# One packed stream for the input and the first weights, and eight warm-up products, at the start of a decoder-trunk kernel

## The chip, the cores and the metric

The kernel runs on one core of a Trainium2 chip, in one launch. The metric is the device time of that launch in microseconds (us). A core has a matrix engine (TensorE, PE in the rows), whose loading of stationary operands is listed apart (PEld), a vector engine (VectorE, DVE), a scalar engine (ScalarE, ACT), a general engine (GpSimd, POOL) and an engine that here only issues transfers (SyncE, SP). Sixteen DMA engines carry the transfers of all queues.

## The reference

The reference is a decoder trunk of two layers over 256 tokens of width 1024, in float32. Layer 0 has full causal attention with 16 heads of 64 (at this length its block-sparse form has one block); layer 1 has sliding-window attention with learned sinks over 4 shared key/value heads. Each is followed by a gated feed-forward part with a causal convolution of width 3.

```
for l in range(2):
    h = rmsnorm(x, attn_norm[l])
    q, k, v = ...                       # layer 0: h @ w_qkv_a; layer 1: own q, shared k and v
    q, k = partial_rope(q), partial_rope(k)
    x = x + attention(q, k, v) @ w_o
    x = x + conv_ffn(rmsnorm(x, ffn_norm[l]), w_up[l], conv_w[l], conv_b[l], w_down[l])
return rmsnorm(x, final_norm)
```

What matters here is the first 40 us: the first normalization, the value half `v` of the first eight heads, and the query and key group of the first four heads.

## The kernel before

**Products.** Each float32 product is made of three products of rounded parts: every operand is split into a high part (rounded, made by ScalarE or VectorE) and a low part (the operand less its high part, made by VectorE). One step of 128 inputs thus takes three products for each of the two token blocks of 128. Tokens are the stationary side, 512 weight columns the moving side.

**Weights.** All weights lie in DRAM as 1 MB units of 128 x 2048 values, in the order of use. A unit is fetched by SP into one of three raw buffers (`fetch`, L151), then split in two or four pieces: `hi_part` (L156) on ScalarE, `lo_part` (L159) on VectorE. The last low piece frees the raw buffer, and the fetch of the unit after next-but-one follows. Units 0 and 1 are the first value half, units 2 and 3 the first query/key group, 4 and 5 the second, 6 and 7 the third.

**Start.** The input lies in DRAM twice: by token (`x`), and transposed, as eight chunks of 128 features x 256 tokens, behind a column of gains (`xg`). `get_x` (L201) and `get_w` (L208) fetch chunks and quarter units: the first two chunks of x on ScalarE's queue, the rest on SP's, x and weights in turn. `warm_up` (L244) multiplies a tile of ones by itself, with no use of the result, six times. `first_parts(c)` (L764) scales and splits chunk c of x and splits its quarter unit; `v_first(c)` (L725) then issues the six products of chunk c. The first parts of x are not yet normalized: the scale of each token is applied when results are copied out, so it has to be known only there.

**What follows the start on the in-order engines.** ScalarE: the high parts of units 2 and 3, then a sine (L801) for the rotary tables, four squares of the input rows (L292, for the normalization), two copies of the value accumulators (`v_out`, L735), then the high parts of units 4 and 5 and the copies of the first query/key group (`qk_out`, L854). GpSimd makes the angles: positions are fetched to `pos_i` (L710), converted (L747), and some twenty small operations on 16 columns end with L763; VectorE takes an absolute value (L798), GpSimd adds a constant (L799), and the sine follows. VectorE: the low parts of units 2 and 3, that absolute value, then the low parts of units 4 and 5 and the rotation of the first group (`rope`, L339: L343, twice L348, L349). Only then can TensorE transpose the rotated group (`to_feature`, L355), four transposes for each token block.

**Who sets the order.** Up to the first attention the order on TensorE, ScalarE and VectorE is that of the code (`manual_schedule`, L703); the steps of splitting, copying and rotating are put into that order by a simple clock that counts the products' nominal time (`tick`, `chain`). From the first attention on a scheduler orders all engines by its own estimates.

```
def part(i, c):
    hi_part(i, c)
    lo_part(i, c)
...
warm_up(6)
for c in range(4):
    first_parts(c)
    v_first(c)
fetch(3)
```

Of the kernel before, what the change touches and what calls it, by code (L numbers as in the profile page):

```python
# [7 lines left out]
F32 = mybir.dt.float32  # L8
F32R = mybir.dt.float32r
I32 = mybir.dt.int32  # L10
AF = mybir.ActivationFunctionType
ALU = mybir.AluOpType
AX = mybir.AxisListType

P = 128
D = 1024
S = 256
NB = S // P
KC = D // P
# [10 lines left out]
UNIT = 2048  # L30
# [27 lines left out]


@with_exitstack  # L60
def trunk(ctx: ExitStack, tc, x, xg, pos, cpk, fin, sinks, w, out):
    nc = tc.nc
    one = ctx.enter_context(tc.tile_pool(name="one", bufs=1))
    qd = ctx.enter_context(tc.tile_pool(name="qd", bufs=15))
    wk = ctx.enter_context(tc.tile_pool(name="wk", bufs=2))
    wp = ctx.enter_context(tc.tile_pool(name="wp", bufs=4))
# [4 lines left out]
    def nm(s):  # L71
        uid[0] += 1
        return f"{s}_{uid[0]}"
# [3 lines left out]
    SKIP, ROUND = 4, 64  # L77

    def spaced(pool, n, dt, tag, name, bufs):
        return pool.tile([P, n + ROUND], dt, tag=tag, name=name, bufs=bufs)[:, SKIP:SKIP + n]  # L80

    def quad(dt=F32R, name="q"):
        return spaced(qd, 4 * S, dt, "q", nm(name), 15).rearrange("p (c t) -> p c t", c=4)
# [7 lines left out]
    def bank(tag):  # L91
        return ps.tile([P, 512], F32, tag=tag, name=nm(tag), bufs=4 if tag == "acc" else 2)

    def f(ap):
        return ap.bitcast(F32)

    def blk(b):
        return slice(b * P, (b + 1) * P)
# [46 lines left out]
    wq = {}  # L145
    done = [0]

    raws = {}
    w_time = [0.0]

    def fetch(i):  # L151
        if i < N_UNITS:
            raws[i] = wp.tile([P, UNIT], F32, tag="raw", name=f"wr{i}", bufs=3)
            nc.sync.dma_start(raws[i], w[i])

    def hi_part(i, c):  # L156
        nc.scalar.activation(wq[i][0][:, c], raws[i][:, c], AF.Copy)  # L157

    def lo_part(i, c):  # L159
        nc.vector.tensor_tensor(out=wq[i][1][:, c], in0=raws[i][:, c], in1=f(wq[i][0][:, c]), op=ALU.subtract)  # L160

    def weights(i):
        wq[i] = (spaced(wp, UNIT, F32R, "hi", f"wh{i}", 4),
                 spaced(wp, UNIT, F32R, "lo", f"wl{i}", 4))
# [29 lines left out]

    x0t = qd.tile([P, 4 * S + ROUND], F32, tag="q", name="x0a", bufs=15)
    x0 = [x0t[:, KC:KC + 4 * S].rearrange("p (c t) -> p c t", c=4), quad(F32, "x0b")]
    g0 = x0t[:, :KC]

    def get_x(q, c, n):  # L201
        if c == 0:
            q.dma_start(x0t[:, :KC + n * S], xg[:, :KC + n * S])
        else:
            q.dma_start(x0[c // 4][:, c % 4:c % 4 + n],
                        xg[:, KC + c * S:KC + (c + n) * S].rearrange("p (c t) -> p c t", c=n))

    def get_w(i, j, n=1):  # L208
        if j == 0:
            raws[i] = wp.tile([P, UNIT], F32, tag="raw", name=f"wr{i}", bufs=3)  # L210
        c = slice(j * 512, (j + n) * 512)
        nc.sync.dma_start(raws[i][:, c], w[i][:, c])

    get_x(nc.scalar, 0, 1)
    get_x(nc.scalar, 1, 1)
    get_w(0, 0)
    get_w(0, 1)

    cp = one.tile([P, NCOL], F32, name="cp")
    pos_i = one.tile([P, NB], I32, name="pos_i")  # L220
# [6 lines left out]
    xr = [one.tile([P, D], F32, name=f"xr{b}") for b in range(NB)]  # L227

    rb = one.tile([P, S], F32, name="rb")
    one.tile([P, 56], F32, name="pad")  # L230


    ident = one.tile([P, P], F32, name="ident")
# [6 lines left out]
    for b in range(NB):  # L240
        t = one.tile([P, NH, HD], F32, name=f"v{b}")
        v_sb.append(t)

    def warm_up(n):  # L244

        if n:
            t = bank("u")
            for _ in range(int(n)):
                nc.tensor.matmul(t[:, :P], ones, ones, start=True, stop=True)
# [4 lines left out]
    def new_hT():  # L254

        return [(quad(), quad()) for _ in range(2)]
# [47 lines left out]
    def hx(hT, c):  # L304
        hi, lo = hT[c // 4]
        return hi[:, c % 4], lo[:, c % 4]
# [382 lines left out]
    def row_bcast(rb, b):  # L689
# [4 lines left out]
        def spread():  # L694
# [7 lines left out]

    manual = ExitStack()  # L703
    manual.enter_context(tc.manual_schedule(engines={mybir.EngineType.PE, mybir.EngineType.Activation,
                                                     mybir.EngineType.DVE}))


    hT = new_hT()
    get_x(nc.sync, 2, 2)
    nc.sync.dma_start(pos_i, pos)  # L710
    get_w(0, 2)
    get_w(0, 3)
    get_x(nc.sync, 4, 2)
    get_w(1, 0)
    get_w(1, 1)
    get_x(nc.sync, 6, 2)
    get_w(1, 2)
    get_w(1, 3)
    get_w(2, 0, 4)
    weights(0)  # L720
    weights(1)
    rs = []
# [2 lines left out]
    def v_first(c):  # L725
        xh, xl = hx(hT, c)
        s_ = slice((c % 4) * 512, (c % 4 + 1) * 512)
        wh, wl = (t[:, s_] for t in wq[c // 4])
        for k, (a, m) in enumerate(((xh, wh), (xl, wh), (xh, wl))):
            for b in range(NB):  # L730
                nc.tensor.matmul(v_acc[b], a[:, blk(b)], m, start=(c == 0 and k == 0), stop=(c == KC - 1 and k == 2))  # L731
        tick(1280)
# [23 lines left out]
    src = ang  # L756
    for c in (TWO_PI_1, TWO_PI_2, TWO_PI_3):
        for k in (kh, kl):
            nc.gpsimd.tensor_scalar(out=kk, in0=k, scalar1=-c, scalar2=None, op0=ALU.mult)
            nc.gpsimd.tensor_tensor(out=rr, in0=kk, in1=src, op=ALU.add)  # L760
            src = rr
    arg = rb[:, 80:112].rearrange("p (k b d) -> p k b d", k=2, b=NB)
    nc.gpsimd.tensor_scalar(out=arg[:, 0], in0=rr, scalar1=PI_IN, scalar2=-PI_IN, op0=ALU.min, op1=ALU.max)  # L763
    def first_parts(c):  # L764
        hi, lo = hx(hT, c)
        src, g = x0[c // 4][:, c % 4], g0[:, c:c + 1]
        s_ = slice((c % 4) * 512, (c % 4 + 1) * 512)
        if c == 0:
            nc.vector.tensor_copy(wq[0][0][:, s_], raws[0][:, s_])
        nc.scalar.activation(hi, src, AF.Copy, scale=g)  # L770
        if c > 0:
            hi_part(c // 4, s_)
        nc.vector.scalar_tensor_tensor(out=lo, in0=src, scalar=g, in1=f(hi), op0=ALU.mult, op1=ALU.subtract)
        lo_part(c // 4, s_)

    warm_up(6)
    for c in range(4):
        first_parts(c)
        v_first(c)
    fetch(3)  # L780
    nc.sync.dma_start(xr[0], x[blk(0)])
    for c in range(4, KC):
        first_parts(c)
        if c < KC - 1:
            v_first(c)
# [18 lines left out]
    for h in range(2):  # L804
        c = slice(h * HALF, (h + 1) * HALF)
# [216 lines left out]
def pack(inp):  # L1022

    import numpy as np

    def k_major(m):
        return m.reshape(m.shape[0] // P, P, m.shape[1])

    units = []
    m = k_major(inp["w_qkv_a"][0])  # L1030
    q, k, v = (m[:, :, i * D:(i + 1) * D] for i in range(3))
    qk = [np.concatenate([q[:, :, g * 256:(g + 1) * 256], k[:, :, g * 256:(g + 1) * 256]], axis=2) for g in range(4)]
    blocks = [v[:, :, :512], qk[0], qk[1], qk[2], v[:, :, 512:], qk[3]]

    def halves(blk):
        for a in range(2):
            units.append(blk[4 * a:4 * a + 4].transpose(1, 0, 2).reshape(P, UNIT))

    def rows2(mat):
        mm = k_major(mat)  # L1040
        for i in range(mm.shape[0] // 2):
            units.append(mm[2 * i:2 * i + 2].transpose(1, 0, 2).reshape(P, UNIT))

    def up(mat):
        mm = k_major(mat).reshape(KC, P, 2, NF, P)
        for i in range(NF):
            units.append(mm[:, :, :, i].transpose(1, 0, 2, 3).reshape(P, UNIT))

    for blk in blocks:
        halves(blk)  # L1050
    rows2(inp["w_o_a"][0])
    up(inp["w_up"][0])
    rows2(inp["w_down"][0])
    halves(k_major(inp["w_kv_b"]))

    order = [(2 * (j // 4) + e) * 4 + j % 4 for j in range(NH // 2) for e in range(2)]
    m = k_major(inp["w_q_b"][0].reshape(D, NH, HD)[:, order].reshape(D, D))
    for g in range(4):
        units.append(m[:, :, g * 256:(g + 1) * 256].transpose(1, 0, 2).reshape(P, UNIT))
    rows2(inp["w_o_b"][0].reshape(NH, HD, D)[order].reshape(D, D))  # L1060
    up(inp["w_up"][1])
    rows2(inp["w_down"][1])
    assert len(units) == N_UNITS
    wpk = np.stack(units)

    def feat(v_):
        return v_.reshape(-1, P).T

    cols = [feat(v_) for v_ in (inp["kv_norm"], inp["attn_norm"][1],
                                inp["ffn_norm"][0], inp["ffn_norm"][1])]  # L1070
    for l in range(2):
        four = np.concatenate([inp["conv_w"][l], inp["conv_b"][l][None]], axis=0)
        cols.append(four.reshape(4, 2 * NF, P).transpose(2, 1, 0).reshape(P, 2 * NF * 4))
    cpk = np.concatenate(cols, axis=1)
    return {
        "x": inp["x"].reshape(S, D),
        "xg": np.concatenate([feat(inp["attn_norm"][0]), inp["x"].reshape(S, KC, P).transpose(2, 1, 0).reshape(P, D * S // P)],
                             axis=1),
        "pos": inp["positions"].reshape(NB, P).T,
        "cpk": cpk,  # L1080
        "fin": inp["final_norm"],
        "sinks": inp["sinks_b"].reshape(NH)[order],
        "w": wpk,
    }
# [19 lines left out]
```

## Time and profile before

| | before |
|---|---|
| median of 3 runs | 586.36 us (586.33 to 586.93) |
| profiled execution | 587.05 us, of it a span of 585.1 us from first to last instruction |
| TensorE busy | 575.0 us, 98% |
| VectorE, ScalarE, GpSimd busy | 430.1, 381.9, 106.3 us |
| moved by DMA | 101.00 MB, mean 173 GB/s |
| TensorE clock granted, mean of the span | 0.998 |

The span is one execution as the hardware profiler saw it. "Busy" of TensorE includes products whose ends are modelled, so that a row of back-to-back products counts as fully busy; how fast they run is read from the distance of their starts.

### The profile page before, as it was taken

What the parts mean: (1) busy time and instruction counts of PE and PEld (TensorE: products, weight loads), DVE (VectorE), ACT (ScalarE), POOL (GpSimd) and SP (SyncE); (2) the same over time, 40 slices, a digit from 0 to 9 for tenths busy, and PEclk for the clock granted to TensorE, in tenths of its full rate; (3) what the DMA queues carried; (4) which work ended last, traced back from release to release, by engine and by line L of the source; (5) the groups of instructions that cost most, each with busy time, mean ns of one, the idle gap of its engine ahead of it and who ended that gap; (6) DMA issues with size and microseconds to landing.
All of it is one profiled execution on the core that took longest, in us unless ns stands there. A gap on an engine that the chain in (4) does not pass through costs nothing.

```text
span 585.1 us, 10179 instructions
## 1 busy us (share of the span) xinstructions
PE 575.0 (98%) x3854; PEld 508.0 (87%) x3854; DVE 430.1 (74%) x928; ACT 381.9 (65%) x768; POOL 106.3 (18%) x124
## 2 busy tenths in 40 slices
PE   8999999999999999999999999999999999999995
PEld 7887777789999999988888977679999999988884
DVE  5598668589977767677669778669987676777714
ACT  5798767578566566565459588758765665656513
POOL 5430001012222222321003000000222223232003
PEclk9999999999999999999999999999999999999999
DMA  8964543314555454548744522243364545446701
GB/s 282 371 225 149 212 144 144 144 38 180 216 171 190 150 211 145 190 171 286 289 143 143 218 73 72 73 145 145 117 244 151 204 150 188 174 160 235 288 0 72
DMA packets 16320, 101.00 MB, mean 173 GB/s; under 512 B 2064, under 2 KB 2448, under 8 KB 4752
## 3 DMA queue, kind: packets, MB, share of 16 engines
q1 hardware_dynamic: 15840, 99.83, 47.6%
q8 instruction: 30, 0.49, 0.3%
q10 hardware_dynamic: 432, 0.53, 0.3%
q14 instruction: 18, 0.15, 0.1%
HBM read 99.30 MB, written 1.05 MB: 172 GB/s over the span
## 4 chain that ended last, share of the span: by engine, by line
PE 65%; DVE 13%; ACT 9%; POOL 7%; issue 5%; DMA 1%; POOLq 0%; DVEq 0%; ACTq 0%
PE acc L520 9%; PE acc L525 9%; PE acc L521 9%; POOL m L652 7%; PE acc L315 5%; PE acc L316 4%; PE acc L317 4%; DVE m L647 4%; DVE m L645 4%; ACT m L641 4%; DVE wl L160 3%; PE t L474 3%; PE acc L731 2%; PE t L453 2%; PE u L404 2%
## 5 line engine op out<-in xcount | busy, mean ns | idle before, releaser
L160 DVE TENSOR_TENSOR wl<-wr,wh 128x1024 fp32r<-128x1024 f32 (+1 forms) x208 | 224.6, 1098 | 33.8 <-ACT wh L157 33.5
L157 ACT ACTIVATE wh<-wr 128x1024 fp32r<-128x1024 f32 (+1 forms) x207 | 192.2, 960 | 32.8 <-PE acc L525 17.1
L652 POOL TENSOR_TENSOR m<-m,m 128x256 f32<-128x256 f32 x44 | 67.6, 1538 | 205.6 <-DVE m L647 177.5
L520 PE MATMUL acc<-wh,q 128*128 128x512 f32 x238 | 94.4, 397 | 0.0
L521 PE MATMUL acc<-wl,q 128*128 128x512 f32 x238 | 92.9, 390 | 0.0
L608 PE MATMUL u<-q,wh 128*128 128x256 f32 x320 | 88.5, 278 | 0.0
L609 PE MATMUL u<-q,wh 128*128 128x256 f32 x320 | 88.0, 275 | 0.0
L610 PE MATMUL u<-q,wl 128*128 128x256 f32 x320 | 88.0, 275 | 0.0
L608 PE MATMUL t<-q,wh 128*128 128x256 f32 x288 | 79.4, 276 | 0.6 <-DVE m L647 0.6
L609 PE MATMUL t<-q,wh 128*128 128x256 f32 x288 | 79.2, 275 | 0.0
L610 PE MATMUL t<-q,wl 128*128 128x256 f32 x288 | 79.2, 275 | 0.0
L525 PE MATMUL acc<-wh,q 128*128 128x512 f32 x238 | 78.9, 392 | 0.0
L656 ACT ACTIVATE q<-m 128x256 fp32r<-128x256 f32 x44 | 18.4, 418 | 82.4 <-POOL m L652 82.4
L608 PEld LDWEIGHTS u<-q,wh 128*128 128x128 f32 x320 | 59.9, 188 | 0.3 <-issue 0.2
L609 PEld LDWEIGHTS u<-q,wh 128*128 128x128 f32 x320 | 60.1, 188 | 0.0
L610 PEld LDWEIGHTS u<-q,wl 128*128 128x128 f32 x320 | 60.1, 188 | 0.0
L315 PE MATMUL acc<-wh,q 128*128 128x512 f32 (+1 forms) x160 | 57.1, 358 | 0.0
L316 PE MATMUL acc<-wl,q 128*128 128x512 f32 (+1 forms) x160 | 56.2, 351 | 0.0
L317 PE MATMUL acc<-wh,q 128*128 128x512 f32 (+1 forms) x160 | 55.9, 349 | 0.0
L608 PEld LDWEIGHTS t<-q,wh 128*128 128x128 f32 x288 | 54.1, 188 | 1.0 <-issue 1.0
L610 PEld LDWEIGHTS t<-q,wl 128*128 128x128 f32 x288 | 54.1, 188 | 0.0
L609 PEld LDWEIGHTS t<-q,wh 128*128 128x128 f32 x288 | 54.1, 188 | 0.0
(153 smaller groups left out, 1028.5 us busy)
## 6 DMA issues: line engine op xcount, KB each, us to landing
wr<-in_w SPq DMA_DIRECT2D x90, 1024.0 KB, 4.8
wr<-in_w SPq DMA_DIRECT2D x8, 256.0 KB, 5.1
xr<-in_x SPq DMA_DIRECT2D x2, 512.0 KB, 9.1
out<-m SPq DMA_DIRECT2D x3, 256.0 KB, 2.1
x0b<-in_xg SPq DMA_DIRECT2D x2, 256.0 KB, 5.2
fin_t<-in_fin SPq DMA_DIRECT2D x1, 512.0 KB, 5.6
x0a<-in_xg SPq DMA_DIRECT2D x1, 256.0 KB, 5.4
out<-m ACTq DMA_DIRECT2D x1, 256.0 KB, 2.1
```

The lines of the kernel that those rows point to most:

```text
L157: nc.scalar.activation(wq[i][0][:, c], raws[i][:, c], AF.Copy)
L160: nc.vector.tensor_tensor(out=wq[i][1][:, c], in0=raws[i][:, c], in1=f(wq[i][0][:, c]), op=ALU.subtract)
L315: nc.tensor.matmul(o, xh[:, blk(b)], wh, start=(c == 0), stop=False)
L316: nc.tensor.matmul(o, xh[:, blk(b)], wl, start=False, stop=False)
L317: nc.tensor.matmul(o, xl[:, blk(b)], wh, start=False, stop=(c == KC - 1))
L520: nc.tensor.matmul(o, ph[:, blk(b)], hi[:, s_], start=first, stop=False)
L521: nc.tensor.matmul(o, ph[:, blk(b)], lo[:, s_], start=False, stop=False)
L525: nc.tensor.matmul(o, pl[:, blk(b)], hi[:, s_], start=False, stop=end)
L608: nc.tensor.matmul(o, hi[:, s_], xh, start=(c == 0), stop=False)
L609: nc.tensor.matmul(o, hi[:, s_], xl, start=False, stop=False)
L610: nc.tensor.matmul(o, lo[:, s_], xh, start=False, stop=(c == KC - 1))
L652: nc.gpsimd.tensor_tensor(out=h, in0=gs, in1=t[1], op=ALU.mult)
```

## The change

The transposed input and units 0 and 1 lie side by side in one array `xw`: the column of gains, then for each chunk its 256 tokens and its 512 weight columns, 768 values a row. Eight chunks come in seven transfers on SP's queue (chunks 4 and 5 together), into the three raw buffers and two other tiles, issued one behind the other ahead of everything else. Nothing is fetched on ScalarE's queue at the start any more. Unit 2 has no raw buffer of its own now and is fetched once chunks 0 and 1 are split, unit 3 once chunks 2 and 3 are. The gains are copied to a tile of their own (`g1`), because the buffer they come in is used again. SP joins the engines whose order is that of the code, and the warm-up has eight products.

```diff
-    get_x(nc.scalar, 0, 1)
-    get_x(nc.scalar, 1, 1)
-    get_w(0, 0)
-    get_w(0, 1)
+    CH = S + 512
+    first = [wp.tile([P, UNIT], F32, tag="raw", name=f"first{i}", bufs=3) for i in range(3)]
+    first += [qd.tile([P, 4 * S + ROUND], F32, tag="q", name=nm("first"), bufs=15) for _ in range(2)]
...
+    def get_chunks(c, n=1):
+        t, at = (first[c // 2], KC * (c == 1) + c % 2 * CH) if c < 6 else (first[c - 3], 0)
+        lo, hi = c * CH + KC * (c > 0), (c + n) * CH + KC
+        nc.sync.dma_start(t[:, at:at + hi - lo], xw[:, lo:hi])
+
+    for c in range(4):
+        get_chunks(c)
+    get_chunks(4, 2)
+    get_chunks(6)
+    get_chunks(7)
+    g0 = first[0][:, :KC]
+    g1 = one.tile([P, KC], F32, name="g1")
...
-    manual.enter_context(tc.manual_schedule(engines={mybir.EngineType.PE, mybir.EngineType.Activation,
-                                                     mybir.EngineType.DVE}))
+    manual.enter_context(tc.manual_schedule(engines={mybir.EngineType.PE, mybir.EngineType.Activation,
+                                                     mybir.EngineType.DVE, mybir.EngineType.SP}))
...
-    get_x(nc.sync, 2, 2)
     nc.sync.dma_start(pos_i, pos)
-    get_w(0, 2)
-    get_w(0, 3)
-    get_x(nc.sync, 4, 2)
...
-    get_w(2, 0, 4)
...
+            nc.vector.tensor_copy(g1, g0)
...
-    warm_up(6)
+    warm_up(8)
     for c in range(4):
         first_parts(c)
         v_first(c)
-    fetch(3)
+        if c % 2:
+            fetch(2 + c // 2)
```

The order of instructions moves at three places that matter below. In the names, `wr5` is the raw buffer of unit 5, `wh5` and `wl5` its high and low parts, `m2` the two tiles of the first query/key group (token blocks 0 and 1), `t` a bank that takes transposes, `acc` an accumulator.

The first is the head of SP's queue. Before:

```order
L212 DMA wr0_74<-in_w 128x512 x2
L205 DMA x0a_70<-in_xg 128x512
L710 DMA pos_i_78<-in_pos 128x2
L212 DMA wr0_74<-in_w 128x512 x2
L205 DMA x0b_1_71<-in_xg 128x512
L212 DMA wr1_107<-in_w 128x512 x2
```

and now:

```order
L210 DMA first0_70<-in_xw 128x776
L210 DMA first0_70<-in_xw 128x768
L210 DMA first1_71<-in_xw 128x768 x2
L210 DMA first2_72<-in_xw 128x1536
L210 DMA first_1_73<-in_xw 128x768
L210 DMA first_2_74<-in_xw 128x768
L710 DMA pos_i_84<-in_pos 128x2
```

The positions were the fourth transfer of this queue and are now the eighth, behind all chunks.

The second is VectorE where it reaches the first rotation (lines move by one: L343 is now L344, and so on). Before:

```order
L160 TENSOR_TENSOR wl5_373<-wr5_247,wh5_372 128x512
L343 TENSOR_TENSOR rb_87<-m2_21_375,cs_265 128x128
L348 TENSOR_TENSOR rb_87<-m2_21_375,sn_266 128x8x8 x2
L349 TENSOR_TENSOR m2_21_375<-rb_87 128x8x16
L160 TENSOR_TENSOR wl5_373<-wr5_247,wh5_372 128x512
L343 TENSOR_TENSOR rb_87<-m2_22_376,cs_265 128x128
L348 TENSOR_TENSOR rb_87<-m2_22_376,sn_266 128x8x8 x2
L160 TENSOR_TENSOR wl5_373<-wr5_247,wh5_372 128x512
L349 TENSOR_TENSOR m2_22_376<-rb_87 128x8x16
```

and now:

```order
L160 TENSOR_TENSOR wl5_372<-wr5_246,wh5_371 128x512 x4
L344 TENSOR_TENSOR rb_93<-m2_22_374,cs_264 128x128
L349 TENSOR_TENSOR rb_93<-m2_22_374,sn_265 128x8x8 x2
L160 TENSOR_TENSOR wl6_431<-wr6_258,wh6_430 128x1024
L350 TENSOR_TENSOR m2_22_374<-rb_93 128x8x16
L344 TENSOR_TENSOR rb_93<-m2_23_375,cs_264 128x128
L349 TENSOR_TENSOR rb_93<-m2_23_375,sn_265 128x8x8 x2
L160 TENSOR_TENSOR wl6_431<-wr6_258,wh6_430 128x1024
L350 TENSOR_TENSOR m2_23_375<-rb_93 128x8x16
```

The first rotation stood behind one quarter of unit 5 and now stands behind all four; half of unit 6 has moved in ahead of the last step of each rotation.

The third is TensorE, where it transposes what was rotated. Before (16 products of units 4 and 5 stand ahead of the first transposes):

```order
L355 MATMUL t_27_416<-ident_89,m2_21_375 128x128 x4
L315 MATMUL acc_25_380<-wh5_372,q_4_100 128x512
L316 MATMUL acc_25_380<-wl5_373,q_4_100 128x512
L317 MATMUL acc_25_380<-wh5_372,q_5_101 128x512
L315 MATMUL acc_25_380<-wh5_372,q_4_100 128x512
L316 MATMUL acc_26_381<-wl4_340,q_2_98 128x512
L317 MATMUL acc_26_381<-wh4_339,q_3_99 128x512
L316 MATMUL acc_25_380<-wl5_373,q_4_100 128x512
L355 MATMUL t_28_421<-ident_89,m2_22_376 128x128 x4
```

and now (15 products ahead):

```order
L356 MATMUL t_28_415<-ident_95,m2_22_374 128x128 x4
L316 MATMUL acc_26_379<-wh5_371,q_5_106 128x512
L317 MATMUL acc_26_379<-wl5_372,q_5_106 128x512
L318 MATMUL acc_26_379<-wh5_371,q_6_107 128x512
L356 MATMUL t_29_420<-ident_95,m2_23_375 128x128 x4
```

The second transposes stood seven products behind the first and now stand three behind them. Later differences of order end some 290 instructions into TensorE's 3,660; from there the two programs are alike.

## Rows read from the trace of the kernel before

**Rows 1.** Waits of TensorE, whole span: us in total, times, longest.
```profile
PE t L355 <- DVE m L349: 0.6, 1, 0.6
```

**Rows 2.** Timeline of TensorE, the start: start us, us, engine, line, instruction.
```profile
1.11 2.93 PE L249 MATMUL u<-ones 128*128 128x128 f32 x12 [1.11 <-DVE warm L225]
5.00 2.07 PE L731 MATMUL acc<-wh,q 128*128 128x512 f32 x4 [0.96 <-ACT q L770]
...
9.44 0.68 PE L731 MATMUL acc<-wl,q 128*128 128x512 f32 x2
...
17.66 0.61 PE L731 MATMUL acc<-wl,q 128*128 128x512 f32 x2
```

**Rows 3.** Timeline of TensorE, at the first transposes of the rotated group.
```profile
29.14 0.61 PE L315 MATMUL acc<-wh,q 128*128 128x512 f32 x2
...
32.77 0.60 PE L355 MATMUL t<-ident,m 128*128 128x128 f32 x4
...
34.81 0.60 PE L355 MATMUL t<-ident,m 128*128 128x128 f32 x4
```

**Rows 4.** Stretches: length, each engine's busy time, clock, DMA share, GB/s.
```profile
0.00:6.00 6.00, 3.93 (x14) 3.46 (x15) 1.62 (x5) 1.99 (x3) 1.88 (x16) 1.00 0.60 168
6.00:14.85 8.85, 8.85 (x33) 7.15 (x32) 6.25 (x13) 6.66 (x14) 6.69 (x15) 1.00 0.99 360
2.50:12.00 9.50, 8.54 (x30) 6.83 (x29) 6.49 (x13) 6.35 (x13) 4.45 (x9) 1.00 0.95 303
12.00:22.00 10.00, 10.00 (x45) 8.09 (x44) 6.96 (x13) 6.46 (x12) 5.73 (x16) 1.00 1.02 420
30.00:570.00 540.00, 538.66 (x3701) 478.01 (x3701) 407.13 (x876) 357.46 (x716) 86.22 (x71) 1.00 0.47 167
```

**Rows 5.** Timeline of GpSimd, from the positions' landing to the angles.
```profile
7.32 0.48 POOL L747 CAST rb<-pos_i 128x2 f32<-128x2 int32 x1 [4.80 <-DMA pos_i<-in_pos]
7.74 0.95 POOL L826 MEMSET kd<- 128x1024 f32 x1
...
10.22 0.31 POOL L838 MEMSET mask<- 128x256 f32 x1
...
11.31 0.42 POOL L839 TENSOR_SCALAR_AFFINE_SELECT mask<-mask 128x128 f32<-128x128 f32 x1
...
18.49 0.52 POOL L763 TENSOR_SCALAR rb<-rb 128x16 f32<-128x16 f32 x1
```

**Rows 6.** Timeline of ScalarE, from unit 2 to units 4 and 5.
```profile
16.97 2.20 ACT L157 ACTIVATE wh<-wr 128x512 fp32r<-128x512 f32 x4 [1.55 <-DMA wr<-in_w]
19.45 2.20 ACT L157 ACTIVATE wh<-wr 128x512 fp32r<-128x512 f32 x4 [0.29 <-DMA wr<-in_w]
23.02 0.23 ACT L801 ACTIVATE rb<-rb 128x32 f32<-128x32 f32 x1 [1.37 <-POOL rb L799]
...
24.84 0.63 ACT L292 ACTIVATE m<-xr 128x512 f32<-128x512 f32 x1 [0.36 <-DMA xr<-in_x]
...
27.81 2.71 ACT L157 ACTIVATE wh<-wr 128x512 fp32r<-128x512 f32 x5
```

**Rows 7.** Timeline of VectorE, around the absolute value and the first rotation.
```profile
22.54 0.17 DVE L798 SCALAR_TENSOR_TENSOR rb<-rb 128x16 f32<-128x16 f32 x1
...
28.47 3.10 DVE L160 TENSOR_TENSOR wl<-wr,wh 128x512 fp32r<-128x512 f32 x5 [1.92 <-ACT wh L157]
31.49 0.29 DVE L343 TENSOR_TENSOR rb<-m,cs 128x128 f32<-128x128 f32 x1
...
32.08 0.29 DVE L349 TENSOR_TENSOR m<-rb 128x128 f32<-128x128 f32 x1
...
37.69 1.22 DVE L160 TENSOR_TENSOR wl<-wr,wh 128x1024 fp32r<-128x1024 f32 x1
```

**Rows 8.** Stretches at the end of the span, columns as in rows 4.
```profile
578.50:582.50 4.00, 0.00 (x0) 0.00 (x0) 2.24 (x8) 1.31 (x4) 1.27 (x2) 1.00 0.27 100
583.00:583.50 0.50, 0.00 (x0) 0.00 (x0) 0.00 (x0) 0.00 (x0) 0.00 (x0) 0.50 0.65 242
```

More of the change, by code (lines that the diff above doesn't have):

```diff
@@ L60, in trunk @@
 @with_exitstack
-def trunk(ctx: ExitStack, tc, x, xg, pos, cpk, fin, sinks, w, out):
+def trunk(ctx: ExitStack, tc, x, xw, pos, cpk, fin, sinks, w, out):
     nc = tc.nc
@@ L193, in need, with chunk @@
         require("w", i)
[L197 to L212, printed above, removed]
-    get_x(nc.scalar, 0, 1)
-    get_x(nc.scalar, 1, 1)
-    get_w(0, 0)
-    get_w(0, 1)
+    CH = S + 512
+    first = [wp.tile([P, UNIT], F32, tag="raw", name=f"first{i}", bufs=3) for i in range(3)]
+    first += [qd.tile([P, 4 * S + ROUND], F32, tag="q", name=nm("first"), bufs=15) for _ in range(2)]
+    def chunk(c):
+        t, at = (first[c // 2], KC * (c < 2) + c % 2 * CH) if c < 6 else (first[c - 3], 0)
+        return t[:, at:at + S], t[:, at + S:at + CH]
+    def get_chunks(c, n=1):
[9 more added lines that the diff above has]
+    g1 = one.tile([P, KC], F32, name="g1")
     cp = one.tile([P, NCOL], F32, name="cp")
@@ L229, in trunk @@
     rb = one.tile([P, S], F32, name="rb")
-    one.tile([P, 56], F32, name="pad")
+    one.tile([P, 48], F32, name="pad")
     ident = one.tile([P, P], F32, name="ident")
@@ L704, in trunk @@
     manual.enter_context(tc.manual_schedule(engines={mybir.EngineType.PE, mybir.EngineType.Activation,
-                                                     mybir.EngineType.DVE}))
+                                                     mybir.EngineType.DVE, mybir.EngineType.SP}))
     hT = new_hT()
-    get_x(nc.sync, 2, 2)
     nc.sync.dma_start(pos_i, pos)
-    get_w(0, 2)
-    get_w(0, 3)
-    get_x(nc.sync, 4, 2)
[L714 to L718, printed above, removed]
-    get_w(2, 0, 4)
     weights(0)
@@ L765, in first_parts @@
         hi, lo = hx(hT, c)
-        src, g = x0[c // 4][:, c % 4], g0[:, c:c + 1]
-        s_ = slice((c % 4) * 512, (c % 4 + 1) * 512)
+        (src, raw), g = chunk(c), (g1 if c > 1 else g0)[:, c:c + 1]
+        wh, wl = (t[:, (c % 4) * 512:(c % 4 + 1) * 512] for t in wq[c // 4])
         if c == 0:
-            nc.vector.tensor_copy(wq[0][0][:, s_], raws[0][:, s_])
+            nc.vector.tensor_copy(wh, raw)
+            nc.vector.tensor_copy(g1, g0)
         nc.scalar.activation(hi, src, AF.Copy, scale=g)
         if c > 0:
-            hi_part(c // 4, s_)
+            nc.scalar.activation(wh, raw, AF.Copy)
         nc.vector.scalar_tensor_tensor(out=lo, in0=src, scalar=g, in1=f(hi), op0=ALU.mult, op1=ALU.subtract)
-        lo_part(c // 4, s_)
-    warm_up(6)
+        nc.vector.tensor_tensor(out=wl, in0=raw, in1=f(wh), op=ALU.subtract)
+    warm_up(8)
     for c in range(4):
@@ L1076, in pack @@
         "x": inp["x"].reshape(S, D),
-        "xg": np.concatenate([feat(inp["attn_norm"][0]), inp["x"].reshape(S, KC, P).transpose(2, 1, 0).reshape(P, D * S // P)],
-                             axis=1),
+        "xw": np.concatenate([feat(inp["attn_norm"][0])] + [
+            t for c in range(KC) for t in (inp["x"].reshape(S, KC, P)[:, c].T, blocks[0][c])], axis=1),
         "pos": inp["positions"].reshape(NB, P).T,
```

## The prediction

> **What bounds the kernel now.** I read the stretches first. From 30 to 570 us TensorE is busy 538.7 of 540 us [rows 4]: the kernel is one stream of products, and what delays the stream early is not made up later. The list of TensorE's waits then tells where the stream ever stops: besides the first microseconds it holds little, but one of its rows is a transpose (L355) that waits 0.6 us for the last step of a rotation on VectorE [rows 1]. So a late rotation does stop TensorE, since it works strictly in order there.
>
> The timeline of the start shows the second thing. The six warm-up products (twelve rows) take 2.93 us and end at 4.04; TensorE idles 0.96 us; from 5.00 to 9.44 it does ten products, 0.444 us each; the 36 from 9.44 to 17.66 take 0.228 us each [rows 2]. 512 columns in 0.43 to 0.44 us are the 1.2 GHz level, half of the later pace, although the clock column shows 1.00 in these stretches [rows 4]. Had the higher level been there from 5.00, ten products would cost 2.2 us less. That is the most that the start can give.
>
> Third, the stretch of the first transposes. From 29.14, 16 products and then four transposes: 32.77 less 29.14, over 16, is 0.227 us a product, so nothing waits; the second transposes at 34.81 come seven products later, which leaves 0.45 us for the four transposes between [rows 3]. On VectorE the last step of the first rotation runs at 32.08 to 32.37 [rows 7]: 0.4 us before it is needed. This is a small margin, and behind it stands a long chain: positions landed at 7.32, angles done at 18.49 + 0.52 = 19.01 [rows 5], absolute value 22.54 [rows 7], sine 23.02, squares, first high part of unit 4 at 27.81 [rows 6], first low part 28.47, rotation 31.49 [rows 7].
>
> **The change, part by part.**
>
> *Warm-up.* Eight products take 8/6 of 2.93, 3.9 us, and end at 5.0, about where the first real product starts now [rows 2]. No time is added; the idle 0.96 us is filled, and the higher clock may come up to 4.4 us earlier. Worth between 0 and 2.2 us at the start; I take 1.5. It is spent before 33 us, as follows.
>
> *Chunks in one queue.* The bytes are the same: 3.15 MB of x and units 0 and 1. Now 168 GB/s for 6.0 us and 360 for the next 8.85 us move 1.01 and 3.19 MB; the mean from 2.5 to 12 is 303, from 12 to 22 it is 420 [rows 4]. With longer rows and no second queue I expect the later pace once the first 1.01 MB are in: 2.14 MB at 420 GB/s take 5.1 us, the last chunk has moved at 11.1. TensorE needs 8 x 6 x 0.228 = 10.9 us from 5.0 at the high clock, so it is just kept fed. The copy of the gains is 128 x 8 values, and lies where VectorE waits for ScalarE: nothing.
>
> *Positions behind the chunks.* In bytes the positions stood behind 1.05 MB (four chunks of x, two quarter units), which had moved at 6.1; they landed at 7.32 [rows 5], 1.2 us after. Unit 2 ends at 4.20 MB, moved at 14.85 [rows 4], and was taken at 16.97 [rows 6], 2.1 us after. The positions now stand behind 3.15 MB: they land at 11.1 + 1.2 = 12.3. The fast bound is 420 GB/s from 2.5, 11.2; the slow one 303 GB/s from 2.5 and 2.1 us, 15.0.
>
> *GpSimd's angles.* From landing to end 11.7 us now, of which the fills L826, L838 and L839 take 0.95 + 0.31 + 0.42 = 1.7 [rows 5]; they now come before the landing. That leaves 10.0, so the angles end at 22.3, not 19.0. Absolute value to sine is 23.02 - 22.54 = 0.5: the sine runs at 22.8 (21.7 to 25.5). Its other releaser is VectorE's work on unit 3: the sine follows that unit's first high part by 23.02 - 19.45 = 3.6 [rows 6]. Unit 3 lies 2.1 MB behind the chunks: 11.1 + 5.0 + 2.1 = 18.2, sine 21.8. So the positions decide, by 1 us, and the faster transfers bring the sine hardly forward (23.0 to 22.8).
>
> *Rotation later in the order.* Here the new order costs. From sine to the first high part of unit 4 now 4.79, of it 0.36 a wait for the input rows [rows 6]; without that 4.4. First low part 0.66 later, and five take 31.49 - 28.47 = 3.02, so 0.60 each [rows 7]. Eight of them, not five, stand ahead of the rotation: 4.83. First two steps of the rotation 0.59, half of unit 6 1.22, last step 0.29 [rows 7]. Sum: sine + 4.4 + 0.66 + 4.83 + 0.59 + 1.22 + 0.29 = sine + 12.0, first transposes at 34.8. The second rotation adds 0.59 + 1.22 + 0.29 = 2.1: second transposes at sine + 14.1 = 36.9.
>
> *Where TensorE stands.* At the present phase it would reach the second transposes, 18 products and four transposes behind 29.14, at 29.14 + 18 x 0.227 + 0.45 = 33.7. The stream is late by sine - 19.6, which is **3.2 us**, some 2.3 to 3.7 of it waiting at the first transposes and the rest at the second. However early the start is, it ends in this wait. What is late next: the third transposes stand 21 products (4.8 us) behind, enough for the splits, copies and one rotation ahead of them (2 half units, 2.4 us; two low parts and a rotation, about 2 us). Then the order is as before.
>
> Sum against the profiled execution: 587.05 + 3.2 = 590.2; that execution lies 0.7 above the median of the runs, 586.36, which gives **589.5**. With the bounds of the sine the forecast's own range is +2.1 to +5.9, 588.4 to 592.3.
>
> **Rivals.**
>
> *The clock falls in the wait.* At the end of the span the last product is over by 578.5; the clock reads 1.00 until 582.5 and 0.50 at 583.0 [rows 8]: 4 us of idling did not lower it, 4.5 did. The forecast's wait is 2.3 to 3.7 us, then three products, then under 1 us. If the level falls and has to be earned again as at the start, 4.44 us at 0.444 instead of 0.227 per product lose 2.2 us: 591.7. Against it: the wait is shorter than the 4 us that changed nothing. Chance 0.12. The Trainium skill ("TensorE: Matmul & The Clock Gate", section "Why this matters for your kernels") warns that an idle gap of this order between bursts of products brings the lower clock back, so by that page the time is 591.7, and by rows 8 it is 589.5; I go by the rows.
>
> *The positions are not held up.* Their 1 KB might land early, near the present 7.32, instead of behind the chunks. Then the sine follows unit 3, at 21.8 or, at 420 GB/s throughout (17.1 + 3.6), 20.7: +1.1 to +2.2, 587.5 to 588.6. For it: it is small. Against it: now it landed in the order of the bytes ahead of it. Chance 0.12.
>
> *The start's gain survives: faster.* The stream gains only if the second rotation is done when TensorE comes, that is with a sine before 19.6; the full 1.5 us of the start (584.9) needs it at 18.1. Unit 3 would have to land by 14.5, 5.25 MB in 12 us from 2.5, some 440 GB/s with no latency, and the positions by 7.6. The trace's best long stretch is 420 [rows 4]. Chance 0.06.
>
> **How the numbers follow.** The forecast has 0.70. About 0.2%, 1.2 us, is what a measurement can tell here. Slower by more: the forecast, the fallen clock, and half of the early positions, less a margin for stalls misread, 0.80. Faster by more: 0.07. Same: 0.13, made of the low end of the early positions and of that margin. The range reaches from 587.2, inside the early positions, to 591.8, which takes in the fallen clock at the likely sine and leaves out the slowest bound.
>
> **What would show it.** Right: the profile after lists TensorE waiting 2 to 4 us in all at L356 for VectorE's L350; the sine (L794) at 22 to 24 with GpSimd as its releaser; the positions' conversion (L738) at 12 to 13; products at 0.23 us well before 9.4; products from 40 us on as many as before and 3 us later. Wrong: no wait at L356, or the conversion before 9, or a stream that waits for unit 2 instead.

## The result, and the profile after

| | before | after |
|---|---|---|
| median of 6 runs each, on the same chip | 586.88 us (586.33 to 587.27) | 590.87 us (590.11 to 592.69) |
| ratio, 95% interval | | 1.0073 (1.0058 to 1.0088) |
| profiled execution | 587.05 us, span 585.1 | 590.83 us, span 588.9 |
| TensorE busy, mean clock | 575.0 us, 0.998 | 575.4 us, 0.995 |

The change costs 4.0 us; the forecast was 3.1 more than before. The longest of TensorE's waits over the whole span, after the change (engine and what waits <- what released it: us in total, times, longest):

```profile
PE t L356 <- DVE m L350: 4.1, 3, 2.6
PE u L250 <- DVE warm L226: 1.1, 1, 1.1
PE acc L316 <- ACT wh L157: 0.7, 1, 0.7
```

One wait of 0.6 us has become three of 4.1 us in all [rows 1]. The third, of 0.63 us, is in layer 1 (at 326.58), as before. Two of them are new, 2.65 and 0.83 us; their places are in the timeline of TensorE after the change: the start, the first and second transposes, and what follows.

```profile
1.11 3.79 PE L250 MATMUL u<-ones 128*128 128x128 f32 x16 [1.11 <-DVE warm L226]
4.84 1.54 PE L722 MATMUL acc<-wh,q 128*128 128x512 f32 x4
6.21 0.61 PE L722 MATMUL acc<-wl,q 128*128 128x512 f32 x2
...
16.21 0.39 PE L316 MATMUL acc<-wh,q 128*128 128x512 f32 x1
...
34.76 0.63 PE L356 MATMUL t<-ident,m 128*128 128x128 f32 x4 [2.65 <-DVE m L350]
...
36.92 1.09 PE L356 MATMUL t<-ident,m 128*128 128x128 f32 x4 [0.83 <-DVE m L350]
37.66 0.78 PE L316 MATMUL acc<-wh,q 128*128 128x512 f32 x1
38.23 0.63 PE L317 MATMUL acc<-wl,q 128*128 128x512 f32 x1
38.66 0.63 PE L318 MATMUL acc<-wh,q 128*128 128x512 f32 x1
39.08 0.63 PE L316 MATMUL acc<-wh,q 128*128 128x512 f32 x1
39.51 0.52 PE L317 MATMUL acc<-wl,q 128*128 128x512 f32 x1
39.87 0.40 PE L318 MATMUL acc<-wh,q 128*128 128x512 f32 x1
```

The start is faster: from 6.21 six products take 1.36 us, 0.23 each, where rows 2 have 0.44 until 9.44. Unit 2's first product starts at 16.21; before the change the last two products of unit 1 started at 17.66 [rows 2], and two of 0.227 us make 18.11 of that. The start gained 1.9 us. At 34.76 all of it and more is gone, in a wait of 2.65 us, and a second one of 0.83. Behind that, the transposes take 1.09 instead of 0.63 and the products stand 0.43 apart until 39.5. The stretches say why (columns as in rows 4; the clock is the third number from the end):

```profile
2.50:12.00 9.50, 9.50 (x42) 7.98 (x41) 6.75 (x14) 6.03 (x13) 1.71 (x5) 1.00 1.01 385
36.00:36.80 0.80, 0.09 (x1) 0.00 (x0) 0.80 (x3) 0.80 (x3) 0.00 (x0) 0.72 0.94 399
36.80:37.50 0.70, 0.58 (x3) 0.61 (x4) 0.70 (x1) 0.70 (x1) 0.69 (x1) 0.50 0.29 117
38.20:39.00 0.80, 0.80 (x3) 0.66 (x2) 0.80 (x2) 0.44 (x1) 0.72 (x2) 0.50 0.56 236
39.80:40.50 0.70, 0.70 (x4) 0.57 (x4) 0.49 (x1) 0.14 (x1) 0.55 (x2) 1.00 1.01 410
```

The granted clock fell to its lower level (0.50, 1.2 GHz) between 36.0 and 36.8 and came back at 39.8. It is not an accident of this execution: the mean granted clock of the span is 0.993 to 0.995 in all six runs, and 0.996 to 0.999 in the listed runs of the kernel before. The transfers are indeed faster: 385 GB/s from 2.5 to 12 instead of 303.

Why the rotation was late, after the change: the positions' conversion, an angle step beside VectorE's splits, one behind them, the last step (GpSimd); unit 3's high parts and the sine (ScalarE); the low parts and the first rotation (VectorE).

```profile
11.75 0.62 POOL L738 CAST rb<-pos_i 128x2 f32<-128x2 int32 x1 [7.72 <-DMA pos_i<-in_pos]
...
18.07 0.58 POOL L750 TENSOR_SCALAR rb<-rb 128x16 f32<-128x16 f32 x1
...
20.91 0.25 POOL L750 TENSOR_SCALAR rb<-rb 128x16 f32<-128x16 f32 x1
...
22.20 0.20 POOL L754 TENSOR_SCALAR rb<-rb 128x16 f32<-128x16 f32 x1
```

```profile
16.55 2.20 ACT L157 ACTIVATE wh<-wr 128x512 fp32r<-128x512 f32 x4 [0.29 <-DMA wr<-in_w]
22.93 0.23 ACT L794 ACTIVATE rb<-rb 128x32 f32<-128x32 f32 x1 [4.17 <-POOL rb L792]
```

```profile
14.73 5.04 DVE L160 TENSOR_TENSOR wl<-wr,wh 128x512 fp32r<-128x512 f32 x8 [0.41 <-ACT wh L157]
...
27.90 4.91 DVE L160 TENSOR_TENSOR wl<-wr,wh 128x512 fp32r<-128x512 f32 x8 [1.91 <-ACT wh L157]
32.72 0.28 DVE L344 TENSOR_TENSOR rb<-m,cs 128x128 f32<-128x128 f32 x1
...
34.33 0.28 DVE L350 TENSOR_TENSOR m<-rb 128x128 f32<-128x128 f32 x1
```

The packed stream brought unit 3 to ScalarE 2.9 us earlier (16.55; 19.45 in rows 6), and VectorE was done with it at 19.77. A sine was possible at about 20.3. It ran at 22.93, as before the change (23.02), and now because GpSimd's angles were late: ScalarE stood idle for 4.17 us. Then eight low parts went ahead of the rotation.

### The profile page after: what moved, and what is told of

Read it like the earlier page. It is cut to its first block, busy times and chain, and to the rows that moved or that the text cites. A ratio compares the mean times of both kernels' runs of the same rounds, so it can differ in the third digit from the quotient of the medians.

```text
span 588.9 us, 10177 instructions
## 1 busy us (share of the span) xinstructions
PE 575.4 (98%) x3858; PEld 508.3 (86%) x3858; DVE 432.7 (73%) x929; ACT 381.6 (65%) x768; POOL 104.4 (18%) x124
## 3 DMA queue, kind: packets, MB, share of 16 engines
HBM read 99.30 MB, written 1.05 MB: 170 GB/s over the span
## 4 chain that ended last, share of the span: by engine, by line
PE 49%; DVE 23%; ACT 9%; POOL 9%; issue 7%; DMA 1%; SPq 1%; POOLq 0%; DVEq 0%; ACTq 0%
PE acc L521 9%; PE acc L526 9%; PE acc L522 9%; POOL m L653 7%; DVE wl L160 7%; DVE m L648 6%; DVE m L646 5%; ACT m L642 4%; PE acc L316 4%; PE acc L318 4%; PE acc L317 3%; PE t L475 3%; PE t L454 2%; ACT q L657 2%; PE u L405 2%
## 5 line engine op out<-in xcount | busy, mean ns | idle before, releaser
L160 DVE TENSOR_TENSOR wl<-wr,wh 128x1024 fp32r<-128x1024 f32 (+1 forms) x200 | 218.8, 1115 | 32.9 <-ACT wh L157 32.7
L157 ACT ACTIVATE wh<-wr 128x1024 fp32r<-128x1024 f32 (+1 forms) x200 | 187.7, 971 | 32.2 <-PE acc L526 19.9
L653 POOL TENSOR_TENSOR m<-m,m 128x256 f32<-128x256 f32 x44 | 65.1, 1479 | 207.7 <-DVE m L648 178.7
L316 PE MATMUL acc<-wh,q 128*128 128x512 f32 (+1 forms) x160 | 58.2, 364 | 0.7 <-ACT wh L157 0.7
L318 PE MATMUL acc<-wh,q 128*128 128x512 f32 (+1 forms) x160 | 56.1, 351 | 0.0
```

Source lines behind the costliest of these rows:

```text
L316: nc.tensor.matmul(o, xh[:, blk(b)], wh, start=(c == 0), stop=False)
L318: nc.tensor.matmul(o, xl[:, blk(b)], wh, start=False, stop=(c == KC - 1))
L653: nc.gpsimd.tensor_tensor(out=h, in0=gs, in1=t[1], op=ALU.mult)
```

## The experiments

The theory: the new start itself gains, and two things beside it lose more, the order (VectorE's rotation behind all of unit 5) and the positions (behind all chunks in their queue); the clock's fall in the resulting wait adds to it. Rivals: the packed stream itself costs; one of the two alone is the loss; the clock fell for another reason. Ratios are against the kernel before, run on the same chip.

**Order kept.** The order of the code is kept on the engines that follow it (TensorE, ScalarE, VectorE and, since the change, SP) until the filling ahead of the first attention is issued, so both rotations stand behind five low parts:

```diff
         fill(lead)
+        if not sink:
+            manual.close()
         state[0] = score(0)
...
-    manual.close()
     attention(qk, ready_a, ...)
```

> The changed kernel, with the order of the code kept on TensorE, ScalarE and VectorE over the two first rotations (it ended just before them). VectorE then does both rotations behind five low parts, not eight, and without half units of unit 6 between. Theory (the late rotation is the loss): sine still at 22.9; first low part 27.9, five of them 3.0 us, rotations of 0.88 us end at 31.8 and 32.7; TensorE comes at 32.1, so it waits under 0.5 us, its clock stays up, and the start's gain is partly left: 0.2 to 0.5 us faster than before. Rival (the packed stream itself costs, the order is a side effect): still 3 us or more slower than before. Rival (positions alone): the same, since the sine does not move.

Measured: 587.85 us, ratio 1.0017 (1.0008 to 1.0026), 1.05 us slower than before.

**Positions early.** They are fetched on ScalarE's queue, which is empty at the start; the order of TensorE and VectorE is that of the changed kernel:

```diff
     pos_i = one.tile([P, NB], I32, name="pos_i")
+    nc.scalar.dma_start(pos_i, pos)
...
-    nc.sync.dma_start(pos_i, pos)
```

> The changed kernel, with the positions fetched on ScalarE's queue at the start; the order on TensorE and VectorE stays the late one. Theory (positions behind the chunks decide the sine, the sine the rotation, the rotation TensorE): conversion before 8, sine right behind unit 3's high and low parts at 20.3 to 20.6, first transposes at 32.2 to 32.5 and second at 34.3 to 34.6 instead of 34.8 and 36.9; TensorE waits 1.3 and 0.8 us. If the clock then holds, 3.4 us faster than the changed kernel, 0.6 us slower than before; if it falls all the same, 1.5 slower than before. Rival (unit 3 or ScalarE decides the sine anyway): no change against the changed kernel, 4 us slower than before.

Measured: 587.07 us, ratio 1.0006 (0.9997 to 1.0015). The conversion ran at 4.48, the sine at 20.59. TensorE's timeline:

```profile
32.54 0.63 PE L357 MATMUL t<-ident,m 128*128 128x128 f32 x4 [1.46 <-DVE m L351]
...
34.70 0.63 PE L357 MATMUL t<-ident,m 128*128 128x128 f32 x4 [0.84 <-DVE m L351]
35.08 0.48 PE L317 MATMUL acc<-wh,q 128*128 128x512 f32 x1
35.39 0.39 PE L318 MATMUL acc<-wl,q 128*128 128x512 f32 x1
35.62 0.39 PE L319 MATMUL acc<-wh,q 128*128 128x512 f32 x1
...
36.31 0.39 PE L319 MATMUL acc<-wh,q 128*128 128x512 f32 x1
```

As expected to within 0.2 us at each place (waits of 1.46 and 0.84), and the products behind are 0.23 apart. In this execution the wait did not bring the clock down. One of the eleven runs (588.64 us, with a mean clock of 0.994; the ten others have 0.996 to 0.999) looks as if it did there, but only one was profiled.

**Both.**

> The two edits together. Theory: sine at 20.4, rotations end at 29.3 and 30.2, TensorE comes to the first transposes at 30.9 and waits for nothing there, nor for the first high part of unit 4; the start's gain of 1.6 to 1.9 us is left whole: 1 to 2 us faster than before. Rival (the start's gain is lost elsewhere, to a later wait for weights or to another rotation): within 0.5 us of before.

Measured: 585.26 us (584.65 to 586.57), ratio 0.9974 (0.9962 to 0.9985): faster than both kernels. The eight transposes start without a wait, and the sixth group of transposes at this line, the same work in each kernel, shows that nearly all of the difference is made by then. In the kernel of both edits:

```profile
30.61 1.03 PE L357 MATMUL t<-ident,m 128*128 128x128 f32 x8
...
62.23 0.66 PE L357 MATMUL t<-ident,m 128*128 128x128 f32 x4
```

before the change, and its one wait for a rotation (the row behind):

```profile
64.17 0.66 PE L355 MATMUL t<-ident,m 128*128 128x128 f32 x4
...
322.70 0.41 PE L355 MATMUL t<-ident,m 128*128 128x128 f32 x2 [0.62 <-DVE m L349]
```

and after it:

```profile
68.07 0.60 PE L356 MATMUL t<-ident,m 128*128 128x128 f32 x4
```

62.23, 64.17 and 68.07: 1.9 us earlier and 3.9 later than before. So four kernels stand in a square (difference to the kernel before, in us):

| | positions behind the chunks | positions early |
|---|---|---|
| rotation late | +4.0 (the change) | +0.3 |
| order kept | +1.05 | -1.5 |

Early positions are worth 3.7 us in the late order and 2.6 in the kept one; the kept order 2.9 and 1.8. The packed stream does not cost; each of the two halves does, and they cost 1.1 us more together than the sum of each alone. Of the four profiles only that of the change shows the clock down at the first transposes, and what this costs, 1.3 us by the last pair of experiments, is about that difference.

The first of these, the kept order, missed its forecast by 1.3 to 1.6 us. Its sine ran at 23.56, and TensorE waited 0.60 and 0.23 us for unit 4's first high and low part, 0.36 at the second transposes and 0.42 at the third. I had left out all but the third of these. The sine at 22.9, taken from one profile, was too early as well: in the seven profiles with the packed stream and late positions it runs at 22.93 (the changed kernel) to 23.87.

**Positions late in the kernel before.**

```diff
     hT = new_hT()
     get_x(nc.sync, 2, 2)
-    nc.sync.dma_start(pos_i, pos)
     get_w(0, 2)
...
+    nc.sync.dma_start(pos_i, pos)
     get_w(2, 0, 4)
```

> The kernel before, with the positions moved behind all its first chunks and quarter units; the order on all other engines is the same. Theory (order and positions act together, the order being the larger part): conversion at 13 instead of 7.3, sine at 23.7 to 24.5 instead of 23.0, TensorE's wait at the first transposes 1.3 to 2.1 us instead of 0.6: 0.7 to 1.5 us slower than before. Rival (the positions alone are the loss): 3 us or more slower than before. Rival (the sine is held by something else): no change.

Measured: 586.86 us, ratio 1.0002 (0.9994 to 1.0011): no change, and the theory's 0.7 to 1.5 missed. The conversion did run at 13.40, the sine at 23.91, 0.9 later, but the input rows that ScalarE had waited 0.36 us for [rows 6] were there by then, and the rotation's last step came only 0.4 later (32.49; 32.08 in rows 7), which is the margin it had. The first transposes started at 33.01 with no wait. The expectation was wrong in a second way: the 0.6 of rows 1 is not at the first transposes at all but at 322.70 (above).

**What the old transfers allow.** The kernel before with eight warm-up products, and then with the positions on ScalarE's queue too:

```diff
-    warm_up(6)
+    warm_up(8)
```

> The kernel before with eight warm-up products instead of six, nothing else; the order is the same on every engine. Theory (the first rotation sets the time in the kernel before too, and what the start gains in front of it is waited away): products at 0.23 us from 6 us on instead of 9.4, TensorE up to 1 us earlier at the first transposes as far as the chunks have landed, the wait there longer by as much: no change, within 0.5 us of before. Rival (the start's gain carries through): 1.5 to 2 us faster.

Measured: 586.77 us, ratio 1.0000 (0.9991 to 1.0009). Right in the time, wrong in the place: the first ten products were done over 1.3 us earlier, but TensorE then waited for the last chunks and unit 2, whose second product started at 18.30 (18.38 in the kernel before). The gain never reached the rotation.

> The kernel before (input and weights in separate transfers on two queues) with eight warm-up products and the positions fetched on ScalarE's queue, behind its two chunks; the order of TensorE and VectorE is the same. It tells what the packed stream itself is worth in the version that beat both kernels. Theory (packing is what brings units 2 and 3 early, and unit 3 then holds the sine): unit 3's high parts start at 19 to 19.5 as before, not at 16.6, sine at 22.5 to 23, no wait and no gain at the first transposes: within 0.5 us of before. Rival (positions and warm-up give the gain, packing nothing): 1 to 1.5 us faster than before.

Measured: 586.42 us, ratio 0.9992 (0.9983 to 1.0001). Unit 3's high parts started at 18.64, the sine ran at 22.21. Behind ScalarE's two chunks the positions came hardly earlier (conversion at 7.22; 7.32 before), but they do not hold the sine here: it follows unit 3's first high part by 3.57 us, as in the kernel before. By the medians about a third of the 1.5 us of the best version comes without the packed transfers; the intervals of the two just overlap. The places are clearer: with the packed transfers the sine runs 2 us earlier (20.19), and the sixth group of transposes stands at 62.23 instead of 63.41.

**Six warm-up products on the packed stream**, in the version of both edits and in the changed kernel:

> The kernel with order kept and positions early, with six warm-up products instead of eight. Theory (the clock at the start is earned by the warm-up, and in this kernel nothing hides it): products at 0.44 us until 8 to 9.5, which costs 1 to 2 us: within 0.7 us of the kernel before. Rival (the packed stream gives the gain, the warm-up nothing): as fast as with eight, 1.5 us faster than before.

Measured: 586.21 us (584.62 to 587.08), ratio 0.9989 (0.9980 to 0.9998): in time what the theory said.

> The changed kernel with six warm-up products instead of eight, the order the same on every engine. Theory (the rotation sets the end, the start only how long TensorE waits for it): the first and second transposes start where they do with eight, at 34.8 and 36.9, whatever the start; no slower than the changed kernel, 3 to 4 us slower than before; if the start is late by 1.5 us or more, the wait is that much shorter and the clock may hold, which gives up to 1 us back. Rival (the start carries through): 1 to 2 us slower than the changed kernel.

Measured: 590.44 us, ratio 1.0064 (1.0050 to 1.0078), the changed kernel's time.

```profile
35.01 1.08 PE L356 MATMUL t<-ident,m 128*128 128x128 f32 x4 [2.65 <-DVE m L350]
...
37.17 1.09 PE L356 MATMUL t<-ident,m 128*128 128x128 f32 x4
...
38.44 0.39 PE L317 MATMUL acc<-wl,q 128*128 128x512 f32 x1
```

The transposes started at 35.01 and 37.17, so the theory held for the changed kernel: the start changes nothing at the end. The clock fell here too, but earlier: the first transposes are already at the lower level (1.08 us for four), and the products are back at 0.23 us from 38.44. The second rotation is late as well, so part of this low spell lies where TensorE would have waited anyway.

In the version of both edits two products fewer cost 0.9 us by the medians, with intervals that just overlap. Its profile, of an execution of 584.62 us, the fastest of its twelve, shows no loss at the start:

```profile
1.11 2.93 PE L251 MATMUL u<-ones 128*128 128x128 f32 x12 [1.11 <-DVE warm L227]
4.95 0.71 PE L724 MATMUL acc<-wh,q 128*128 128x512 f32 x2 [0.91 <-ACT q L764]
```

Two products 0.23 apart at 4.95: the higher level was there after six. The kernel before shows 0.44 until 9.44 after the same six [rows 2]. Over all profiles here: of four with six warm-up products two had the faster pace (0.23 to 0.28) from 5 us on and two not before 9.4; of ten with eight all had it by 7.5. In these profiles eight made the early rise more certain. That this alone is the 0.9 us was not shown: only one execution of that kernel was profiled.

**The wait alone.** The kept order, with the first step of the first rotation repeated, so that TensorE's wait grows and nothing else moves up to there:

```diff
-    def rope(t, nh, b):
+    def rope(t, nh, b, times=1):
...
-        nc.vector.tensor_tensor(out=ta, in0=t[:, :, 0:ROT], in1=c, op=ALU.mult)
+        for _ in range(times):
+            nc.vector.tensor_tensor(out=ta, in0=t[:, :, 0:ROT], in1=c, op=ALU.mult)
...
-              (750.0, lambda: rope(t.rearrange("p (h d) -> p h d", d=HD), 2 * n, b)),
+              (750.0, lambda: rope(t.rearrange("p (h d) -> p h d", d=HD), 2 * n, b, 14 if key == ("qk", 0) and b == 0 else 1)),
```

> The kernel of the kept order (late positions), with the first step of the first rotation done 14 times over instead of once (same operands, same result): 13 more of some 0.2 us on VectorE, so that TensorE's wait at the first transposes grows by about 2.6 us with nothing else moved on the engines up to there. Theory of the clock (an idle of about 2.5 us and a short one behind it bring it down, at some 1 us): the time grows by 2.6 + 1 = 3.6 us against the kept order, 4.6 slower than before, and products behind the second transposes stand 0.43 us apart with a clock of 0.50. Rival (the clock fell in the changed kernel for another reason than the wait): 2.6 us against the kept order, 3.6 slower than before, products 0.23 us apart.

Measured: 593.55 us, ratio 1.0119 (1.0106 to 1.0132), 5.7 slower than the kept order (3.6 forecast). The 14 steps took 4.53 us, some 0.32 each and not 0.2, so the wait was 4.08 us; the eight transposes behind it took 2.08 us (1.03 in the version of both edits) and the first products were 0.43 apart, as the theory said. The time is no clean price of this: layer 1 uses the same helper with the same key twice, so the repeats run there too. Before that, at a transpose of the layer's input (306.50; 301.91 in the kept order), the stream is 4.6 us behind.

The same with eight products of the tile of ones ahead of the transposes:

```diff
+        for _ in range(8 if key == ("qk", 0) and b == 0 else 0):
+            nc.tensor.matmul(pt[:, :P], ones, ones, start=True, stop=True)
         for j in range(n):
             nc.tensor.transpose(pt[:, j * P:(j + 1) * P], t[:, j * P:(j + 1) * P], ident)
```

> The same as the one with the long wait, and eight products of the tile of ones, with no use of their result, on TensorE ahead of the first transposes, in the wait. Theory: the wait is as long for the stream, 2.6 us, but the clock stays at 1.00 and products behind stand 0.23 us apart: 2.6 us against the kept order, 3.6 slower than before, and 1 us faster than the long wait left empty. Rival (the clock is not a matter of the wait): the same time as the empty wait.

Measured: 596.3 us. This one does not decide: the eight products fill 1.95 us of it, 2.28 us of idling were left, and the clock fell all the same; and the products ran again in layer 1, like the repeats, at 322.08 and 332.84. With nine repeats the wait is nearly as long as in the changed kernel (2.46 us; 2.65), and ten products fill it but for 0.21 us; what counts is read at the first transposes.

> As the long wait, with the first step of the rotation done 9 times over: the repeats took 0.35 us each there (4.53 us for 14), so eight more are 2.8 us and TensorE's wait at the first transposes about 2.7 us, what the changed kernel has (2.65). Read in the profile, not in the time, since the scheduler orders later work otherwise. Theory (a wait of this length alone brings the clock down): eight transposes take 2.1 us instead of 1.0, the first products behind them stand 0.43 us apart, the clock reads 0.50 there. Rival (it took the second, short wait too, or a longer one): eight transposes in 1.0 us, products 0.23 us apart at once.

```profile
34.78 0.63 PE L357 MATMUL t<-ident,m 128*128 128x128 f32 x4 [2.46 <-DVE m L351]
35.78 0.63 PE L357 MATMUL t<-ident,m 128*128 128x128 f32 x4 [0.37 <-DVE m L351]
36.17 0.60 PE L316 MATMUL acc<-wh,q 128*128 128x512 f32 x1
36.57 0.63 PE L317 MATMUL acc<-wl,q 128*128 128x512 f32 x1
...
39.55 0.50 PE L318 MATMUL acc<-wh,q 128*128 128x512 f32 x1
```

> The same, with ten products of the tile of ones ahead of the first transposes: eight of them took 1.95 us where the wait was filled before, so ten take 2.4 us and leave TensorE idle for 0.3 us. Read in the profile. Theory: the transposes start as late as without them, but the eight take 1.0 us and the products behind stand 0.23 us apart with the clock at 1.00, so the ninth product behind the transposes comes about 1.8 us earlier than without them. Rival (the fall is not for want of work on TensorE): the same low pace as without them.

```profile
32.47 2.39 PE L357 MATMUL t<-ones 128*128 128x128 f32 x20
35.07 0.63 PE L359 MATMUL t<-ident,m 128*128 128x128 f32 x4 [0.21 <-DVE m L351]
36.07 0.63 PE L359 MATMUL t<-ident,m 128*128 128x128 f32 x4 [0.37 <-DVE m L351]
36.45 0.48 PE L316 MATMUL acc<-wh,q 128*128 128x512 f32 x1
36.77 0.40 PE L317 MATMUL acc<-wl,q 128*128 128x512 f32 x1
...
38.53 0.39 PE L318 MATMUL acc<-wh,q 128*128 128x512 f32 x1
```

The stretch from 36 to 40 us, with the wait left empty and with it filled (columns as in rows 4):

```profile
36.00:40.00 4.00, 4.00 (x14) 3.29 (x13) 4.00 (x6) 2.54 (x4) 2.56 (x4) 0.57 0.24 55
36.00:40.00 4.00, 3.93 (x19) 3.12 (x20) 4.00 (x6) 3.60 (x6) 2.28 (x4) 1.00 0.12 33
```

The two executions (591.53 and 594.8 us, one of each kernel) differ later, by the uses in layer 1 among others. Up to the second transposes TensorE's work is late by the same rotation in both. From those transposes to the ninth product behind them it is 39.55 - 35.78 = 3.77 us with the wait left empty, and 38.53 - 36.07 = 2.46 with it filled. The clock reads 0.57 and 1.00. So the wait is what brings the clock down; over all profiles, it fell in the five with a wait of 2.28 us or more at the first transposes and in none of the nine others. Here that costs **1.3 us**, less than the 1.8 expected, since the transposes themselves still ran at the higher level.

## Why the prediction was right, and where a term was off

- *Start.* 1.9 us gained in this execution (1.1 to 1.9 in the profiles with the packed stream and eight warm-up products), 1.5 taken. "Spent before 33 us" held: it went into the wait.
- *Positions.* Conversion at 11.75 (12.3 forecast, and 12 to 13 named as the sign of it), angles done at 22.40 (22.3), sine at 22.93 (22.8), released by GpSimd. Half a microsecond of earlier landing was lost again on GpSimd: 10.65 us for the angles, not 10.0. That the sine came within 0.1 us is therefore partly luck: two errors of opposite sign, and the earliest sine of the profiles with this stream and late positions.
- *Rotation.* Sine + 11.8 and + 14.0 instead of 12.0 and 14.1; transposes at 34.76 and 36.92 (34.8 and 36.9). The second ones stand 3.2 us behind the 33.7 they had without waits, the forecast's number.
- *Its evidence.* The sentence that rows 1 show the stream stopped "there" by a rotation was wrong of the place: that wait is at 322.70. The conclusion, that a rotation later than its 0.4 us of margin stops TensorE, rests on rows 3 and 7 alone, and the runs bore it out.
- *A wait left out.* TensorE waited 0.67 and 0.22 us for unit 4's first parts, since they hang on the late sine too. It cost nothing more: without it the wait at the transposes would have been longer by as much.
- *The clock: the mis-sized term.* The forecast put it at nothing ("the wait is shorter than the 4 us that changed nothing", rows 8) and gave the fall to a rival, at 0.12. It fell. Size: in the changed kernel the second transposes to the sixth product behind them took 39.87 - 36.92 = 2.95 us; in the kernel with early positions, same order and same second wait, 36.31 - 34.70 = 1.61; so 1.3 us, which the last pair of experiments confirms. It is kept: at the sixth group of transposes (68.07; 64.50 with early positions) these two are 3.57 us apart, of which 2.22 were there at the second. The step that failed is the reading of rows 8: they show how long an engine that stays idle keeps the higher level, and I took that for how long it may idle without harm. In this case the fall came between 36.0 and 36.8, more than a microsecond after TensorE had begun to work again at 34.76. The size is not the same in every execution: in the changed kernel with six warm-up products, where the clock fell as the wait ended, the same six products took 39.35 - 37.17 = 2.18 us, 0.6 too long instead of 1.3. The forecast's range holds 590.87 because it took this rival in. The warning of the Trainium skill ("TensorE: Matmul & The Clock Gate", section "Why this matters for your kernels") against idle gaps of this order was the better guide: by it the time was 591.7, and the trace agrees with its direction. Its size there, 2.2 us, was mine, from the start, and too large.
- *Sum.* 3.2 + 1.3 = 4.5 at 40 us; 3.9 at the transposes of 68.07. Some 0.6 is given back between, where the orders still differ; this was not followed up.
- *The other rivals.* The positions were held up behind the chunks, as the forecast had it: issued at 4.21, they took 7.5 us to land, and 3.6 on ScalarE's empty queue. The start's gain could survive, as the experiments show, but only with a sine at 20 and the order kept; with the changed kernel's own queue and order the sine had to come before 19.6 and did not.

## What to carry to other kernels

A faster load at the start pays only when the longest chain behind it starts earlier too: look for the smallest transfer that a chain hangs on (here 1 KB of positions) and give it a queue in which nothing stands ahead of it. Where a scheduler orders work by estimates, compare the order at the first place where the in-order engine meets that chain, and hold it by hand if it moved; here each of the two was worth 2 to 4 us, against 1.9 us that the stream itself gained. And price a new wait of some microseconds on TensorE with a spell at half the pace behind it, not with its length alone.

## What the runs showed of the hardware that I had not expected

- *The clock can fall late.* Waits of 2.28, 2.46, 2.65 (twice) and 4.08 us were each followed by a clock of 0.50. After the wait of 2.46 and one of 2.65 it fell only when TensorE had been at work again for over a microsecond (from 34.78; the products are slow from 36.17); in the three others the first transposes were already slow. Waits of 1.46 and 0.84 close together were not followed by a fall in the one execution profiled. The lower level stayed for about 3 us (to 39.8 after the change).
- *GpSimd beside VectorE.* While VectorE ran its low parts without a gap (14.73 to 19.77), GpSimd's steps on 16 columns took 0.44 to 0.74 us (0.58 at 18.07), about one for each low part of 0.6; once VectorE was idle the same step took 0.25 (20.91). The Trainium skill ("GPSIMD Engine Reference", section "1. Specifications") names contention of the two for their memory interface when VectorE's instruction reads two inputs from the on-chip memory SBUF, as the low part does; this trace agrees (0.58 beside the low parts, 0.25 without).
- *The clock column at the start.* It reads 1.00 in stretches where products stand 0.44 us apart [rows 2, 4]; there the pace of the products tells the level, not the column.
